# Attention units in chains: one unit's outputs and the next unit's scores in one TensorE visit, the sample tokens' attention behind all units, loads kept behind the product ahead of them

## The chip, the cores and the metric

The kernel runs on one core of a Trainium2 chip. The metric is device time in microseconds (us) of one launch. Three runs of the kernel before gave 830.59, 831.8 and 834.57 us; the median is 831.8. A core has TensorE (PE in the profile; its weight loads PEld), VectorE (DVE), ScalarE (ACT), GpSimd (POOL) and SyncE (SP, which issues most DMAs here). Each of them takes its own instructions in order.

## The reference

One layer of a hybrid decoder over 1024 prompt tokens and 8 × 4 sample tokens, width 1024. What matters here, cut from it:

```
h, gate = adaln_in(x, c, w_ada, b_ada, g_norm)            # normalised rows
(mq, mk, mv, mi, mf, mo, mz, aq, ak, av, az, gm, ga) = split_in(h @ w_in)
y_m, C, n, m = mlstm_branch(mq, mk, mv, mi, mf, mo, mz, C0, n0, m0, ...)   # chunks of 128, 4 heads
o = attention(aq, ak, av)   # 8 query heads on 2 key heads, window 128, a sink per head
y_a = o * silu(az)
u = sigmoid(gm) * (y_m @ w_mo) + sigmoid(ga) * (y_a @ w_ao)
x = x + gate * (u @ w_o)
```

Prompt attention goes in blocks of 128 tokens: a block's 128 queries see the block and the one before it. The sample tokens attend to a cache of 128 keys per sample and to themselves; their attention is a computation of its own. Their 32 rows also pass through each of the products with `w_in`.

## The kernel before, in words

**The products.** Nearly all of TensorE's time goes into `h @ w_in` and the two output products. Each fp32 operand is split into two fp32r parts (hi and lo), and each product is three fp32r matmuls with 128 × 128 weights and 288 to 512 columns. In the order of the profile: keys and values `ak`, `av` of the attention, its four groups of queries `aq`, the first four of the mLSTM heads' projections (`mq`, `mk`, `mv`) as plain products (`job`, line 569, `piece` at 525ff, tiles `g_...`), and then, from about 207 us, pairs of weight blocks in a seven-product scheme (`block_products`, line 1516, accumulators `bw`, `bx`, `by`, `bz`): the remaining head projections (`head_in`), eight pairs `ga`/`gm` (`gate`), two of `az` (`query_gate`), four of `mo`/`mz` (`head_gate`). A pair's four raw weight blocks (256 KB each, tiles `wr_...`) are loaded by its `load`; its `samples` multiplies them raw, in fp32, with the sample rows (accumulator `smp`, then `smpo`), and DVE and ACT form the split parts from them afterwards.

**What stands between the products.** Small fp32 matmuls and transposes are put between two products, in *visits*. A `Side` object (line 113) decides when. Work is written as generators that yield a lag and the names of PSUM banks ("a", "b", "o", two buffers each) that the next step needs; they run in streams, "a" (attention: at most 5 at a time, a new one 8.0 us after the last), "m" (mLSTM heads), "s" (sample attention), "g" and "x" (others). `tick` (line 140) is called after each product of a group. It has its own clock, `side.now`, which `mm` and `tr` move forward by nominal durations, lets a visit come at least 1.5 us after the last, and takes every generator whose lag is over and whose banks are free. A bank is held after a visit for `HOLD` (line 110: 2.0 us for "a" and "b", 4.0 for "o") or, where the step named "+", for 6.0 us (line 152). PE's instructions run on the chip in the order in which they are emitted (`in_order`); DVE, ACT and SP instructions of this part are placed by a scheduler that knows the data and bank dependencies, and `no_sync` (line 202) gives it an order to keep between two instructions, without a semaphore.

**An attention unit** (`unit`, line 826) is two blocks of 128 queries of one query group g, so there are 16. Its steps: four loads of queries, keys and values (tiles `uqv`, `ukv`); *scores*, 8 matmuls into two "a" banks (`sc`), behind which DVE adds the mask and takes the row maximum, four instructions, and the scores' bank is free; two yields in which ACT takes the exponentials and DVE and ACT normalise; *transposes* of the weights (`pt`, one "b" and one "o" bank); and *outputs*, 16 matmuls into an "o" bank (`oT`), behind which ACT copies them out and POOL issues the store. `queries(g)` adds the four units of a group as four generators to stream "a". From the first paired head on (`sc_bank[:] = po, "o+"` in `head_jobs`, line 1023) scores go to "o" banks, as the block products take the "a" banks, and at most three generators of stream "a" run at a time.

**Sample attention** (`sample_attention`, line 911) is one generator in stream "s": it loads the two halves of the key and value caches, transposes the keys, and does scores, softmax and outputs for the sample tokens. In the profile it stands between about 140 and 196 us. Its result `osm` is read by the `samples` step of the two `query_gate` pairs; `hook` (line 2013) holds those until all units and the sample attention are done.

**Heads.** `head` (line 1038) does one mLSTM head in groups of up to three chunks: loads `hq`, `hk`, `hv`, `et`, `qw`; `prep` (DVE: mask added to `et`, `qw` times q); transposes `tk`, `tv`; `S`; `U` with the state chain `C` on DVE; numerators `n` (also `sn` for samples).

**Loads.** `dma` calls `issue` (line 258), which puts a `dma_start` on SP. Where the scheduler puts it among SP's instructions follows from its buffer (a pool of 50 `half` tiles and pools for raw weights) and its data, so a load can stand far ahead of the product that was emitted before it.

Of the kernel before, what the change touches and what calls it, by code (L numbers as in the profile page):

```python
# [112 lines left out]
class Side:  # L113
# [26 lines left out]
    def tick(self, visit=False):  # L140
        self.each()
        for st in self.streams.values():
            if st["wait"] and len(st["live"]) < st["max"] and self.now >= st["next"]:
                self.begin(st)
        used, visit = set(), visit or self.now >= self.last + self.quiet
        for item in sorted((i for st in self.streams.values() for i in st["live"]), key=lambda i: i[1]):
            banks = set(item[2])
            if self.now < item[1] or used & banks or (banks and not visit) or any(self.now < self.free.get(b, 0) for b in banks):
                continue
            used |= banks  # L150
            for b in banks:
                self.free[b] = self.now + (6.0 if "+" in banks else HOLD[b])
            n = self.products
            self.step(item)
            if self.products > n:
                self.last = self.now
# [17 lines left out]
def body(tc, a):  # L174
    nc = tc.nc
    with ExitStack() as ctx:
# [23 lines left out]
        last = {}  # L200
# [53 lines left out]
        def dma(out, in_, late=False):  # L254
            stores(in_.tensor)
            issue(out, in_, late)

        def issue(out, in_, late=False, eng=None):
            ins = (eng or nc.sync).dma_start(out, in_)  # L259
            ins = getattr(ins, "ins", ins)  # L260
            if late:
                no_sync(ins, free)
                free.clear()
            free.append(ins)
# [556 lines left out]
        osm = cp.tile([128, NH, NS], F32, name="osm")  # L821
        yaD = [dp.tile([128, T], F32, name=f"yaD{g}") for g in range(4)]

        sc_bank = [pa, "a"]

        def unit(g, b0):
            sink = at["sink"]
            los = [128 if b == 0 else 0 for b in (b0, b0 + 1)]
            n0 = 1 if b0 == 0 else 0
            qv, kv_ = ht([128, 4, 128], "uqv"), ht([128, 4, 128], "ukv")  # L830
            q, kT = qv[:, 0:2].rearrange("p c e -> p (c e)"), kv_[:, 0:3].rearrange("p c e -> p (c e)")
            vn = kv_[:, 3], qv[:, 2], qv[:, 3]
            dma(q, qD[g][:, b0 * 128:b0 * 128 + 256])
            dma(kT[:, n0 * 128:], kD[:, (b0 - 1 + n0) * 128:(b0 + 2) * 128])
            dma(qv[:, 2:4], vnD[:, b0:b0 + 2])
            if b0:
                dma(vn[0], vnD[:, b0 - 1])
            yield 12.0, sc_bank[1]
            p = [ht([128, 2, 256], f"p{kv}") for kv in range(2)]
            mx = sm([128, 4], "mx", 3)  # L840
            scs = [sc_bank[0]([128, 2, 256], f"sc{g}_{b0}_{kv}") for kv in range(2)]
            for i, lo in enumerate(los):
                qc, kc = slice(i * 128, i * 128 + 128), slice(i * 128 + lo, i * 128 + 256)
                for kv, r in enumerate(half_rows):
                    mm(scs[kv][:, i, lo:], q[r, qc], kT[r, kc], start=True, stop=True, share=2)
            for kv in range(2):
                for i, lo in enumerate(los):
                    V.tensor_tensor_reduce(p[kv][:, i, lo:], scs[kv][:, i, lo:], amask[:, lo:], 1.0, sink[:, kv, g:g + 1],
                                           ALU.add, ALU.max, accum_out=mx[:, 2 * kv + i:2 * kv + i + 1])
            nmx = sm([128, 8], "nmx", 3)  # L850
            V.tensor_scalar(nmx[:, 0:4], mx, -1.0, None, op0=ALU.mult)
            v2 = lambda t: t.rearrange("p (k i) -> p k i", i=2)
            V.tensor_tensor(v2(nmx[:, 4:8]), sink[:, :, g:g + 1].to_broadcast((128, 2, 2)), v2(mx), op=ALU.subtract)
            yield 2.5, ""
            den = sm([128, 4], "den", 3)
            S.activation(nmx[:, 4:8], nmx[:, 4:8], AF.Exp)
            for kv in range(2):
                for i, lo in enumerate(los):
                    j = 2 * kv + i
                    S.activation(p[kv][:, i, lo:], p[kv][:, i, lo:], AF.Exp, bias=nmx[:, j:j + 1],  # L860
                                 accum_out=den[:, j:j + 1])
            yield 3.0, ""
            V.tensor_tensor(den, den, nmx[:, 4:8], op=ALU.add)
            V.reciprocal(den, den)
            for kv in range(2):
                for i, lo in enumerate(los):
                    j = 2 * kv + i
                    if kv:
                        S.activation(p[kv][:, i, lo:], p[kv][:, i, lo:], AF.Copy, scale=den[:, j:j + 1])
                    else:  # L870
                        V.tensor_scalar(p[kv][:, i, lo:], p[kv][:, i, lo:], den[:, j:j + 1], None, op0=ALU.mult)
            yield 7.6, "b"
            pT = [t.rearrange("p i (j e) -> p (i j) e", e=128) for t in p]
            for kv in range(2):
                pt = (pb, po)[kv]([128, 4, 128], f"pt{g}_{b0}_{kv}")
                for j in range(n0, 4):
                    tr(pt[:, j], p[kv][:, j // 2, j % 2 * 128:j % 2 * 128 + 128], ident)
                if kv:
                    V.tensor_copy(pT[kv][:, n0:], pt[:, n0:])
                else:  # L880
                    S.copy(pT[kv][:, n0:], pt[:, n0:])
            yield 5.0, "o"
            oT = po([128, 2, 128], f"oT{g}_{b0}")
            for j in range(n0, 4):
                i, hf = divmod(j, 2)
                for kv in range(2):
                    r = slice(64 * kv, 64 * kv + 64)
                    mm(oT[r, i], vn[i + hf][:, r], pT[kv][:, j], start=(hf == 0 or b0 + i == 0), stop=(hf == 1))
            c0 = b0 * 128
            o = qv[:, 0:2].rearrange("p c e -> p (c e)")  # L890
            S.copy(o, oT.rearrange("p c e -> p (c e)"))
            issue(oD[g][:, c0:c0 + 256], o, eng=nc.gpsimd)
            units_done.append((g, b0))

        def queries(g):
            cs = at["rope"]

            def ev_q(p, acc, c0, n):
                q = ht([128, 384], "aq")[:, :n]
                S.activation(q, acc[:, :n], AF.Copy, scale=0.125)  # L900
                t = rope(q, cs[p], n, ht([128, 384], "aqr"), qD[g], c0)
                if p == 2:
                    v3 = lambda x, r: x[r, 256:288].rearrange("p (b t) -> p b t", t=NT)
                    for kv, r in enumerate(half_rows):
                        V.tensor_tensor(at["qpad"][r, :, kv, g], v3(q, r), v3(t, r), op=ALU.add)

            job(("aq", g), ev_q)
            for b0 in (0, 2, 4, 6):
                side.add("a", unit(g, b0))

        def sample_attention():
            qpad, vns, kTs = at["qpad"], at["vns"], at["kTs"]
            kc, vc = ([ht([128, 4, 128], f"{n}{u}") for u in range(2)] for n in ("kc", "vc"))
            smask = ht([128, 2, WIN + NS], "smask")
            sinkr = cp.tile([128, 1], F32, name="sinkr")
            for u in range(2):
                dma(kc[u], a["cache_k"][:, 4 * u:4 * u + 4])
                dma(vc[u], a["cache_v"][:, 4 * u:4 * u + 4])
            dma(smask, a["smask"])
            dma(sinkr, a["sink_rows"])  # L920
            yield 12.0, "b"
# [27 lines left out]
            V.reciprocal(den, den)  # L949
            for u in range(2):  # L950
                V.tensor_scalar(p[:, u], p[:, u], den[:, u:u + 1], None, op0=ALU.mult)
            yield 10.0, "b"
            pt = pb([128, 4, 128], "pts")
            for u in range(2):
# [45 lines left out]
        def head_jobs(h):  # L1000
# [15 lines left out]
            for n, dst, smp, scale in (("mq", q, qs, float(128 ** -0.5)), ("mk", k, ks, 1.0), ("mv", v, vs, 1.0)):  # L1016
                if (n, h) not in order:
                    return
                i = order.index((n, h)) - order.index(None)
                if i == -1:  # L1020
                    plain_ends.append(True)
                    side.finish("g")
                    sc_bank[:] = po, "o+"
                    side.streams["a"]["max"] = 3
                    next(work)
                job((n, h), keep(dst, smp, scale, "s"), (lambda: next(work)) if i == -1 else None)
                head_part(h, 2)
# [901 lines left out]
        side.add("m", gates(gp, zg, gbias), "")  # L1929
        side.add("a", kv_turn(), "b")  # L1930
        V.on = S.on = False

        gbD, gsD = dp.tile([1, D], F32, name="gbD"), dp.tile([NS, D], F32, name="gsD")

# [78 lines left out]
        def hook(n, i):  # L2013
# [9 lines left out]
                side.add("x", att_sums(LOADS.index((n, i))))  # L2023
            if n == len(pairs) - 1:
                next(att, None)

        OUT_WEIGHTS = 5
        LOADS = [(len(pairs) - 2, 7), (len(pairs) - 1, 5)]
# [348 lines left out]
```

## Time and profile before

| | us |
|---|---|
| median of three runs | 831.8 |
| the profiled execution | 830.97 |
| its span (first to last instruction) | 829.2 |
| DVE busy | 592.7 |
| ACT busy | 420.6 |
| POOL busy | 67.5 |
| DMA, mean over the span | 186 GB/s |

The mean granted TensorE clock of the profiled execution was 0.996 of full speed. A row of a timeline reads: start, duration, engine, line, operation, out<-in, the shape of the weight tile (rows\*columns of the array), the moving operand, count; in brackets, idle time of the engine just before and what ended it. A matmul's duration overlaps the next one's, so its cost is read from start to start. L271 and L276 are the lines of the helpers `mm` and `tr`, L220 that of DVE, ACT and POOL calls, L259 that of DMA issues, so groups are told apart by their tiles.

### The profile page before, as it was taken

How to read it: one execution, taken by the hardware profiler on the slowest of the kernel's cores; microseconds unless marked ns; L12 is line 12 of the kernel's file. 1: busy time of each engine (PE TensorE's matmuls, PEld its weight loads, DVE VectorE, ACT ScalarE, POOL GpSimd, SP SyncE). 2: the span in 40 equal slices, each digit the busy share in tenths (PEclk: the TensorE clock that was granted, in tenths of full speed). 3: DMA queues.
4: the chain of work that ended last, by engine and by line, in shares of the span. 5: the costliest groups of instructions: out<-in, count | busy, mean ns of one | idle time of the engine just before them, and what ended most of it. 6: DMA issues, size and time to landing. Idle time of an engine off the chain costs nothing. (4 is left out here: it accounts for less than half of the span.)

```text
span 829.2 us, 15039 instructions
## 1 busy us (share of the span) xinstructions
PE 810.1 (98%) x5129; PEld 670.8 (81%) x5129; DVE 592.7 (71%) x1479; ACT 420.6 (51%) x1030; POOL 67.5 (8%) x128
## 2 busy tenths in 40 slices
PE   6999999999999999999899999999999999999996
PEld 3779897888788788888788878888888789987775
DVE  4889886647556456475567786797669988964776
ACT  5664365565474564555455454554446654334343
POOL 0120000000000001000001010000002104250000
PEclk9999999999999999999999999999999999999999
DMA  9997756346435324468756354464336785543533
GB/s 332 379 359 239 200 186 212 118 151 219 141 111 186 118 81 150 139 242 279 256 191 211 105 169 150 147 205 142 103 120 197 228 295 186 191 146 123 202 109 108
DMA packets 106689, 153.96 MB, mean 186 GB/s; under 512 B 20448, under 2 KB 54368, under 8 KB 106580
## 3 DMA queue, kind: packets, MB, share of 16 engines
q1 hardware_dynamic: 100964, 142.25, 52.2%
q10 hardware_dynamic: 4176, 6.56, 2.2%
q0 software_dynamic: 1472, 4.20, 1.4%
q8 instruction: 40, 0.66, 0.3%
q14 instruction: 37, 0.30, 0.1%
HBM read 109.22 MB, written 44.75 MB: 186 GB/s over the span
## 5 line engine op out<-in xcount | busy, mean ns | idle before, releaser
L220 ACT ACTIVATE p<-p,nmx 128x256 f32<-128x256 f32 (+1 forms) x64 | 31.0, 485 | 12.4 <-DVE nmx L220 12.1
L271 PE MATMUL g_aq<-h_h,wh_aq 128*128 128x384 f32 (+1 forms) x96 | 32.2, 336 | 0.0
L271 PE MATMUL g_aq<-h_h,wl_aq 128*128 128x384 f32 (+1 forms) x96 | 30.9, 322 | 0.0
L271 PE MATMUL g_aq<-h_l,wh_aq 128*128 128x384 f32 (+1 forms) x96 | 30.8, 321 | 0.0
L271 PE MATMUL g_w_mo<-ym_l,wh_w_mo 128*128 128x384 f32 (+1 forms) x96 | 30.8, 321 | 0.0
L271 PE MATMUL g_w_mo<-ym_h,wh_w_mo 128*128 128x384 f32 (+1 forms) x96 | 30.8, 321 | 0.0
L271 PE MATMUL g_w_mo<-ym_l,wl_w_mo 128*128 128x384 f32 (+1 forms) x96 | 30.8, 321 | 0.0
L220 DVE CUSTOM_DVE_ANT_0 p<-sc,cst,sink 128x256 f32<-128x256 f32 (+1 forms) x64 | 26.2, 464 | 5.3 <-PE sc L271 5.2
L259 POOL DMA_DIRECT2D oD<-uqv x16 | 8.9, 554 | 183.2 <-ACT uqv L220 161.0
L220 DVE COPY p<-pt 128x512 f32<-128x512 f32 (+1 forms) x16 | 10.5, 656 | 13.6 <-PE pt L276 13.6
L271 PEld LDWEIGHTS g_aq<-h_h,wh_aq 128*128 128x128 f32 x96 | 18.0, 188 | 2.5 <-issue 1.5
L271 PEld LDWEIGHTS g_w_mo<-ym_l,wh_w_mo 128*128 128x128 f32 x96 | 18.0, 188 | 0.0
L271 PEld LDWEIGHTS g_aq<-h_l,wh_aq 128*128 128x128 f32 x96 | 18.0, 188 | 0.0
L271 PEld LDWEIGHTS g_w_mo<-ym_h,wh_w_mo 128*128 128x128 f32 x96 | 18.0, 188 | 0.0
L271 PE MATMUL sc<-ukv,uqv 64*128 64x256 f32 (+1 forms) x128 | 18.0, 390 | 0.0
L271 PEld LDWEIGHTS g_w_mo<-ym_l,wl_w_mo 128*128 128x128 f32 x96 | 18.0, 188 | 0.0
L271 PEld LDWEIGHTS g_aq<-h_h,wl_aq 128*128 128x128 f32 x96 | 18.0, 188 | 0.0
L220 ACT ACTIVATE p<-p,den 128x256 f32<-128x256 f32 (+1 forms) x32 | 14.5, 491 | 5.7 <-DVE den L220 5.6
L220 DVE TENSOR_TENSOR et<-et,S 128x384 f32<-128x384 f32 (+1 forms) x12 | 6.1, 510 | 15.6 <-PE S L271 12.9
L220 ACT ACTIVATE sq<-rows_h 128x512 f32<-128x512 f32 (+2 forms) x14 | 8.2, 582 | 17.8 <-issue 12.0
L271 PE MATMUL g_mq<-h_h,wh_mq 128*128 128x384 f32 (+1 forms) x48 | 16.8, 349 | 0.3 <-ACT mk L220 0.3
L276 PE MATMUL pt<-cst,p 128*128 128x128 f32 x120 | 16.4, 277 | 0.5 <-DVE mx L220 0.5
(2073 smaller groups left out, 2842.4 us busy)
## 6 DMA issues: line engine op xcount, KB each, us to landing
x<-xT SPq DMA_DIRECT2D x16, 256.0 KB, 5.4
early_h<-w_ada SPq DMA_DIRECT2D x8, 512.0 KB, 9.0
adar_ga<-w_ada SPq DMA_DIRECT2D x16, 256.0 KB, 3.9
wr_ga<-w SPq DMA_DIRECT2D x16, 256.0 KB, 2.9
wr_gm<-w SPq DMA_DIRECT2D x16, 256.0 KB, 3.0
taD<-gt SPq DMA_DIRECT2D x16, 256.0 KB, 2.0
tmD<-gt SPq DMA_DIRECT2D x16, 256.0 KB, 5.5
wor<-w_out SPq DMA_DIRECT2D x16, 256.0 KB, 4.9
```

Of the source, the lines that this page charges most:

```text
L220: ins = f(*args, **kw)
L259: ins = (eng or nc.sync).dma_start(out, in_)
L271: in_order(nc.tensor.matmul(out, lhsT, rhs, start=start, stop=stop, skip_group_check=more))
L276: in_order(nc.tensor.transpose(out, in_, idn))
```

## The change

It changes six things and no arithmetic.

- `queries` no longer adds four generators per group; it appends four units to a list, and for g = 0, 1, 2 adds one *chain* to stream "a".
- A chain (`unit_chain`, new) runs units one after another. When a unit's transposes are done and the list holds another unit, the chain takes it and starts it (its loads go out), and then does the outputs of the first and the scores of the second in one step, which asks for the banks of both; what remains is the second unit's steps. The third chain takes no new unit once the paired heads have begun.
- Outputs that share a visit go to `sc_bank[2]`: an "o" bank as before, and a "b" bank once the scores themselves go to "o" banks.
- The 6.0 us of hold for "+" now hold for bank "o" alone, not for the other bank of the same visit.
- `sample_attention` waits until all 16 units are done; it issues the loads of the value cache only behind its softmax, no longer with those of the keys.
- From the end of the attention's keys and values to the start of the second pair from the end, each load on SP gets a `no_sync` order behind the last PE instruction emitted before it (`paced`).

In the two programs' orders, the scores of the first unit stand where they stood, 13 visits hold `oT` and `sc` one behind the other (none before), the last `oT` stands near 300 us of a nominal count (319 before), and sample attention near 324 to 365 us.

```
-                self.free[b] = self.now + (6.0 if "+" in banks else HOLD[b])
+                self.free[b] = self.now + (6.0 if b == "o" and "+" in banks else HOLD[b])
...
+        paced = []
+
         def issue(out, in_, late=False, eng=None):
             ins = (eng or nc.sync).dma_start(out, in_)
             ins = getattr(ins, "ins", ins)
+            if eng is None and paced:
+                no_sync(ins, [last["PE"]])
...
-        sc_bank = [pa, "a"]
-
-        def unit(g, b0):
+        sc_bank = [pa, "a", po, "o"]
+        units = []
+
+        def unit(g, b0, joined):
...
             yield 5.0, "o"
-            oT = po([128, 2, 128], f"oT{g}_{b0}")
+            oT = (sc_bank[2] if joined else po)([128, 2, 128], f"oT{g}_{b0}")
...
+        def unit_chain(i):
+            v = w = None
+            while v or len(units_done) < 16:
+                if v is None:
+                    if not units or (i == 2 and plain_ends):
+                        yield 1.0, ""
+                        continue
+                    joined = []
+                    v = unit(*units.pop(0), joined)
+                    next(v)
+                    yield 12.0, sc_bank[1]
+                yield next(v)
+                yield next(v)
+                step = next(v)
+                if units and not (i == 2 and plain_ends):
+                    after = []
+                    w = unit(*units.pop(0), after)
+                    next(w)
+                    joined.append(True)
+                yield step
+                lag, _ = next(v)
+                yield lag, sc_bank[1] + sc_bank[3] if w else "o"
+                for _ in v:
+                    pass
+                v, w = w, None
+                if v:
+                    joined = after
+
...
             for b0 in (0, 2, 4, 6):
-                side.add("a", unit(g, b0))
+                units.append((g, b0))
+            if g < 3:
+                side.add("a", unit_chain(g))
 
         def sample_attention():
             qpad, vns, kTs = at["qpad"], at["vns"], at["kTs"]
-            kc, vc = ([ht([128, 4, 128], f"{n}{u}") for u in range(2)] for n in ("kc", "vc"))
+            while len(units_done) < 16:
+                yield 1.0, ""
+            kc = [ht([128, 4, 128], f"kc{u}") for u in range(2)]
...
                 dma(kc[u], a["cache_k"][:, 4 * u:4 * u + 4])
-                dma(vc[u], a["cache_v"][:, 4 * u:4 * u + 4])
...
+            vc = [ht([128, 4, 128], f"vc{u}") for u in range(2)]
+            for u in range(2):
+                dma(vc[u], a["cache_v"][:, 4 * u:4 * u + 4])
...
-                    sc_bank[:] = po, "o+"
+                    sc_bank[:] = po, "o+", pb, "b"
...
         V.on = S.on = False
+        paced.append(True)
...
+            if n == len(pairs) - 2:
+                paced.clear()
```

## Prediction

> **What bounds the kernel now.** I read the page's first part, then the waits of TensorE (PE), then windows, then the timeline where the windows show a dip.
>
> ```profile
> span 829.2 us, 15039 instructions
> PE 810.1 (98%) x5129; PEld 670.8 (81%) x5129; DVE 592.7 (71%) x1479; ACT 420.6 (51%) x1030; POOL 67.5 (8%) x128
> ```
>
> PE is busy for 810.1 of 829.2 us; no other engine passes 71%. So the time is what PE's instructions take in the order they stand in, plus its stalls. The waits (in total, times, longest) give the stalls:
>
> ```profile
> PE S L271 <- DVE C L220: 2.3, 1, 2.3
> PE bw L271 <- ACT bw L220: 0.7, 1, 0.7
> PE pt L276 <- DVE mx L220: 0.5, 1, 0.5
> PE g_mq L271 <- ACT mk L220: 0.3, 1, 0.3
> ```
>
> Apart from the start, which the change doesn't touch, these four are nearly all of it. Windows (PE is the first busy column; granted clock, DMA share and GB/s stand last) show what the first of them cost:
>
> ```profile
> 100.00:120.00 20.00, 20.00 (x138) 17.98 (x138) 18.44 (x71) 10.31 (x32) 0.71 (x1) 1.00 0.61 197
> 180.00:200.00 20.00, 19.98 (x189) 15.96 (x186) 12.36 (x44) 9.99 (x33) 1.31 (x4) 1.00 0.69 221
> 402.00:408.00 6.00, 3.74 (x25) 3.38 (x24) 1.85 (x4) 1.73 (x8) 0.10 (x1) 0.90 0.69 242
> 408.00:412.00 4.00, 4.00 (x15) 3.17 (x14) 2.32 (x4) 2.22 (x5) 0.00 (x0) 0.72 0.57 210
> ```
>
> PE is full elsewhere (the first two rows). From 402 to 408 it idles for 6.00 − 3.74 = 2.26 us, and the granted clock then falls: 0.90 over 6 us loses 0.60 us, 0.72 over 4 us loses 1.12. The dip cost 2.26 + 0.60 + 1.12 = **4.0 us**.
>
> **The change part by part.** PE gets the same 5129 instructions. In the two programs' instruction orders, set side by side, only their places differ, with those of the loads. So there are three terms: visits of small fp32 groups that merge or split, stalls that go, stalls that come.
>
> *Merged visits.* A visit interrupts the fp32r products. Scores alone, then outputs alone (start, duration, both in us):
>
> ```profile
> 122.60 0.34 PE L271 MATMUL g_mq<-h_h,wl_mq 128*128 128x384 f32 x1
> 122.87 1.13 PE L271 MATMUL sc<-ukv,uqv 64*128 64x256 f32 x8
> 123.94 0.44 PE L271 MATMUL g_mq<-h_h,wh_mq 128*128 128x384 f32 x1
> 124.22 0.33 PE L271 MATMUL g_mq<-h_l,wh_mq 128*128 128x384 f32 x1
> ```
>
> ```profile
> 126.32 0.33 PE L271 MATMUL g_mq<-h_l,wh_mq 128*128 128x384 f32 x1
> 126.49 0.34 PE L271 MATMUL g_mq<-h_h,wl_mq 128*128 128x384 f32 x1
> 126.76 0.44 PE L271 MATMUL oT<-p,ukv 128*64 128x128 f32 x4
> 127.03 0.83 PE L271 MATMUL oT<-p,uqv 128*64 128x128 f32 x12
> 127.78 0.44 PE L271 MATMUL g_mq<-h_h,wh_mq 128*128 128x384 f32 x1
> 128.06 0.33 PE L271 MATMUL g_mq<-h_l,wh_mq 128*128 128x384 f32 x1
> ```
>
> Product to product is 0.17 us (126.32 to 126.49). The step into either group is 0.27 and the first step after it 0.28. So each border costs 0.10, and two visits have four borders. Two groups put into one visit:
>
> ```profile
> 143.73 1.07 PE L271 MATMUL ada_ga<-adar_ga,c 128*32 128x512 f32 x8
> 144.73 1.14 PE L271 MATMUL sc<-ukv,uqv 64*128 64x256 f32 x8
> 145.79 0.44 PE L271 MATMUL g_mk<-h_h,wh_mk 128*128 128x384 f32 x1
> ```
>
> Scores behind other matmuls take 145.79 − 144.73 = 1.06; alone they take 123.94 − 122.87 = 1.07. The inner border is free, and a merge saves two borders, 0.2 us. After the change 13 visits hold outputs and the next unit's scores; before none does. No row shows that pair, so I take 0.2 from the nearest one, with 0 as the lower end and 0.4 (all four borders) as the upper. Three merges of the sample sums with numerators, or of like kind, are lost: −13 × 0.2 + 3 × 0.2 = **−2.0 us**.
>
> Some 14 lost adjacencies have transposes at one side, and these I price at nothing:
>
> ```profile
> 132.31 0.34 PE L271 MATMUL g_mq<-h_h,wl_mq 128*128 128x384 f32 x1
> 132.48 1.04 PE L276 MATMUL pt<-cst,p 128*128 128x128 f32 x8
> 133.44 0.93 PE L271 MATMUL sc<-ukv,uqv 64*128 64x128 f32 x8
> ```
>
> Products enter transposes in 0.17 us, the plain step, so a visit of transposes alone has no border to pay at its front. If I am wrong by 0.05 each, it is 0.7 us.
>
> One page speaks against this term. The Trainium skill, "TensorEngine Tiling (Array Packing)", section "Key Properties", says that a change of tiling mode (the tile shapes behind the "*" above) drains TensorE. By that rule outputs (128\*64) to scores (64\*128) is a switch as well; two visits have four switches and the merged one three, so the 13 merges would save half. The row of 144.73 disagrees, as 128\*32 to 64\*128 cost nothing there; but no run here shows this pair.
>
> *The stall at 404 goes.* Its cause, DVE's and SP's instructions ahead of S:
>
> ```profile
> 404.54 0.56 DVE L220 TENSOR_TENSOR et<-et,cst 128x384 f32<-128x384 f32 x1 [2.07 <-DMA et<-nmd]
> 405.92 0.56 DVE L220 TENSOR_TENSOR qw<-qw,hq 128x384 f32<-128x384 f32 x1 [0.83 <-DMA qw<-wid]
> 406.40 0.34 DVE L220 SCALAR_TENSOR_TENSOR C<-C,dec,U 128x129 f32<-128x129 f32 x1
> ```
>
> ```profile
> 398.84 0.32 SPq L259 DMA_DIRECT2D et<-nmd  x1
> 399.25 0.38 SPq L259 DMA_DIRECT2D qw<-wid  x1
> ```
>
> S needs the bank that C reads last; C stands in DVE's order behind two preparations whose loads were issued at 398.84 and 399.25, and which started at 404.54 and 405.92: 5.7 and 6.7 us from issue to use. In the changed order C still stands behind such a pair, but their loads come about 13 us before S needs the bank (they came 404.4 − 398.84 = 5.5 us before). 13 is above 6.7, so the wait goes: −4.0. What is late next there is the visit after it, counted below. The two smaller waits go too, as their visits no longer stand like that: pt (−0.5, transposes right behind scores whose bank they need) and g_mq (−0.3). Together **−4.8 us**.
>
> *New stalls.* Side by side, nine places remain where PE's next group follows what it waits for with less room than its chain took before: scores at the end of the key products, where DVE is full (18.44 of 20 us in the row of 100 to 120); one visit with outputs, scores and transposes like the one of 0.5; head products behind evictions on ACT and DVE; three numerator visits around 390 to 400; and the first sample sums. The four rows of waits above show what such places cost when they cost anything: 0.3 to 0.7 leaving out the big one. I take 0.3, the lowest, as several will be covered: 9 × 0.3 = **+2.7 us**; ends 0 and 9 × 0.7 = 6.3.
>
> *Loads placed behind the product ahead.* SP's issues are tied to the last PE instruction in program order. For the gate weights this cuts the lead:
>
> ```profile
> L271 PE MATMUL smp<-wr_gm,c x128: 272/273/297, 308.9 to 486.8; 128*32 128x128 f32 x128
> ```
>
> ```profile
> L259 SPq DMA_DIRECT2D wr_gm<-w x16: 328/333/424, 275.7 to 467.0; - x16
> wr_gm<-w SPq DMA_DIRECT2D x16, 256.0 KB, 3.0
> tmD<-gt SPq DMA_DIRECT2D x16, 256.0 KB, 5.5
> wor<-w_out SPq DMA_DIRECT2D x16, 256.0 KB, 4.9
> ```
>
> ```profile
> 401.92 0.39 PE L271 MATMUL bw<-t2h,wh_pgate__4792 128*128 128x512 f32 x1
> 402.15 0.39 PE L271 MATMUL bw<-t2l,wh_pgate__4792 128*128 128x512 f32 x1
> ```
>
> Before, the first load goes out at 275.7 for sums at 308.9 (33 us), the last at 467.0 for 486.8 (20 us). After, by the order, a pair's last load stands 15 products (15 × 0.23 = 3.5 us, by the rows of 401.92 and 402.15) ahead of its sums at two visits (near 407 and 567 us), some 4.3 us at a third, 5.6 at a fourth, and 6 to 11 at the others. A load takes 3.0 us to land, so I count nothing beyond the 0.3 above. Loads amid others took 4.9 and 5.5, and the four of a pair now go out within 2 to 3 us of each other: that is the slower rival. The same tie takes loads out of the first 100 us, where no stall of PE is put down to a load: nothing.
>
> *Sample attention* moves from about 140 to 196 us to about 324 to 365. Its result is first needed with the query gates, after 500 us, so it costs its visits only, as before; the unit work ends some 20 us earlier, in windows where DVE has room (12.36 of 20 from 180 to 200). The freed hold on a bank, the split cache loads: nothing, since no PE instruction is added. If that cover failed, scores would wait on DVE, which the first of the nine places prices.
>
> **The sum.** 830.97 (profiled execution; 829.2 of span and 1.8 around it) − 2.0 − 4.8 + 2.7 = 826.9. The median of the runs, 831.8, lies 0.8 above that execution; I add half of it: **827.3 us**. What can be told from no change is about 0.5%, so faster begins at 827.6 and slower at 836.0.
>
> **Rivals.**
> *A, my forecast*, 825 to 829.5: new stalls between 0.5 and 5 us.
> *B, merges save nothing*: +0.6 instead of −2.0, so 829.9. For it: no row of this pair; against: the row of 144.73. The page's rule lies halfway, 828.6, inside A.
> *C, the big stall comes back* at another numerator visit, since DVE still takes preparations and C in order: 827.3 + 4.0 = 831.3. For it: the same instructions, still in one order; against: the 13 us of lead. This is the case in which the change does not do what it seems to.
> *D, slower: late gate weights.* Each pair's four loads share the engines, and the last lands last. If it takes 6.0 us, the four visits with the least lead stall 2.5, 2.5, 1.7 and 0.4 us, 7.1 together, and two of these idles are as long as the one at 404 and bring its slow clock (0.60 + 1.12 each): 827.3 + 7.1 + 3.4 = 837.8. Below some 5.7 us of landing it stays inside 0.5%. For it: 4.9 and 5.5 beside these loads; against: 3.0 as their own median, and SP isn't held by PE when it runs, so that it may be ahead of its place in the order.
> *E, no new stall*: 827.3 − 2.7 = 824.6, and 822.6 if a merge saves 0.4.
>
> On D's price, the Trainium skill, "TensorE: Matmul & The Clock Gate", section "What's actually happening", has the clock halve after an idle window of about 3.4 us. The trace disagrees on the length: 2.26 us of idle was enough here.
>
> **Chances.** A 0.43, E 0.20, D 0.17, B 0.10, C 0.10. Faster: all of E and 0.24 of A, 0.44. Same: the rest of A, B, C and 0.02 of D, 0.41. Slower: 0.15 of D. The range runs from 823.5 (E with part of the larger saving) to 835.0, leaving out D and the low end of E.
>
> **What would show it.** In the changed trace: outputs and scores in one visit with the scores' part at about 1.07 us (B: 1.2 or more with the step behind it); no wait of S on C near 400; waits of PE in a list of parts of 0.2 to 0.7, 2 to 3 us in total; smp without a wait on DMA. A wait of smp on wr_gm or wr_ga, or a granted clock below 1.00 between 300 and 490, would make it wrong toward D; a PE wait above 2 us in any other place, toward C.

## The result, and the profile after

The changed kernel takes **836.4 us** in the median (835.48 to 838.18, 8 runs); the kernel before, measured beside it, 831.65 (829.35 to 834.57). The ratio is 1.0061, 95% interval 1.0046 to 1.0077: it is slower by 0.6%, clear of noise. The forecast of 827.3 us missed in size and in sign, and the time lies above its range, which ended at 835.0.

The page of the changed kernel, span and busy time:

```profile
span 834.5 us, 15050 instructions
PE 811.4 (97%) x5129; PEld 671.0 (80%) x5129; DVE 591.1 (71%) x1479; ACT 418.9 (50%) x1030; POOL 68.0 (8%) x128
```

TensorE still has the same 5129 instructions and is busy nearly throughout; the span grew by 5.3 us. Its waits (total, times, longest), those above 0.2 us without the start:

```profile
PE bw L275 <- ACT bw L220: 3.3, 2, 2.6
PE pt L280 <- DVE mx L220: 2.8, 2, 2.1
PE bx L275 <- ACT gt L220: 1.0, 1, 1.0
...
PE by L275 <- DVE gt L220: 0.5, 1, 0.5
PE smp L275 <- DMA wr_gm<-w: 0.4, 2, 0.3
```

The wait of S on C is gone, as forecast. In its place stand one of 2.6 us (bw, near 529 us) and one of 2.1 (transposes pt, near 256), and a few smaller ones. The wait at 256 brought the slow clock, that is a stretch with a granted clock below 1.00, as the wait at 404 did before (granted clock in the third column from the right):

```profile
256.00:260.00 4.00, 3.25 (x13) 2.65 (x14) 2.95 (x12) 1.76 (x5) 0.00 (x0) 0.76 0.17 66
260.00:264.00 4.00, 4.00 (x22) 3.49 (x21) 0.97 (x4) 3.66 (x15) 0.10 (x1) 0.82 0.00 0
520.00:540.00 20.00, 17.40 (x119) 13.36 (x117) 13.96 (x32) 8.89 (x20) 0.00 (x0) 1.00 0.45 142
```

0.24 and 0.18 of 4 us each are 1.7 us lost behind the idle time; at 529 the clock stayed full (third row). The merged visit, one of 13:

```profile
187.23 0.34 PE L275 MATMUL g_mq<-h_h,wl_mq 128*128 128x384 f32 x1
187.50 0.44 PE L275 MATMUL oT<-p,ukv 128*64 128x128 f32 x4
187.76 0.83 PE L275 MATMUL oT<-p,uqv 128*64 128x128 f32 x12
188.52 1.14 PE L275 MATMUL sc<-ukv,uqv 64*128 64x256 f32 x8
189.58 0.44 PE L275 MATMUL g_mq<-h_h,wh_mq 128*128 128x384 f32 x1
189.87 0.34 PE L275 MATMUL g_mq<-h_l,wh_mq 128*128 128x384 f32 x1
```

The scores take 189.58 − 188.52 = 1.06 us here too: the border from outputs to scores costs nothing. Above plain steps of 0.17 the visit costs 189.87 − 187.23 − 0.34 = 2.30 us. The two visits of before (122.60 to 124.22, 126.49 to 128.06) cost 1.28 + 1.23 = 2.51. So a merge saves 0.21.

Where the 5.3 us of span come from, each item from the waits, the timeline and the windows of the two traces (a visit is priced against the cheapest showing of the same visit in any run; the two totals of the first line are such sums, which no view shows; what counts is their difference):

| | us |
|---|---|
| visits, all of them, at their cheapest: 142.5 before, 140.8 after | −1.7 |
| the wait at 404 and its slow clock | −4.0 |
| the waits of pt at 288 and g_mq at 136 | −0.8 |
| transposes at 256: wait 2.1, restart 0.2, slow clock 1.7 | +4.0 |
| bw at 529 | +2.6 |
| bx at 367 | +1.0 |
| numerators, S and by, 398 to 410 | +1.1 |
| sample sums at 416 | +1.2 |
| scores and transposes at 122 and 181 | +1.4 |
| start, up to the first product | +0.3 |
| sum | +5.1 |

0.2 us are left over. So the expected gains came, 6.5 us of them, and 11.3 us of new stalls ate them.

### The profile page after: what moved, and what is told of

Its sections match the earlier page's. It is cut to its first block, busy times and chain, and to the rows that moved or that the text cites. A ratio compares the mean times of both kernels' runs of the same rounds, so it can differ in the third digit from the quotient of the medians.

```text
span 834.5 us, 15050 instructions
## 1 busy us (share of the span) xinstructions
PE 811.4 (97%) x5129; PEld 671.0 (80%) x5129; DVE 591.1 (71%) x1479; ACT 418.9 (50%) x1030; POOL 68.0 (8%) x128
## 5 line engine op out<-in xcount | busy, mean ns | idle before, releaser
L220 DVE COPY p<-pt 128x512 f32<-128x512 f32 (+1 forms) x16 | 10.5, 655 | 10.9 <-PE pt L280 10.8
L280 PEld LDWEIGHTS pt<-cst,p 128*128 128x128 f32 x120 | 13.8, 140 | 4.9 <-DVE mx L220 3.3
```

The source lines that it names most:

```text
L220: ins = f(*args, **kw)
L280: in_order(nc.tensor.transpose(out, in_, idn))
```

## The experiments

Two theories at the outset. **Collisions**: the new order puts groups of TensorE right behind unfinished work of VectorE and ScalarE, and each place is a matter of a few products. **Late loads**: the tie of the loads to the product ahead is what costs. All times are medians, with the ratio to the kernel before measured beside it. Waits and rows are those of one profiled execution of each run.

### Parts alone and parts undone

**No tie.** Edit:

```
-        paced.append(True)
```

> The changed kernel with the loads no longer tied to the product ahead of them; TensorE's order is that of the changed kernel. Collisions (the new order puts groups right behind unfinished work of VectorE and ScalarE; loads have little to do with it): the waits at 256 (2.1 us and a slow clock of 1.8) and at 529 (2.6) stay, only the sums' waits on their weights go (0.4 shown, about 1 in all): 834.5 to 836.5. Late loads (the tie is what costs): most of the 4.8 us over the kernel before goes: 831 to 832, and below that by the merges.

832.1 us, ratio 1.0018 (1.0005 to 1.0030). Inside the changed kernel the tie costs some 4 us, so the forecast by collisions missed. The wait at 256 stayed, though (1.9 us, without the slow clock this time, which is 1.7 of the 4 in the two traces), and that of 2.6 at 529 became two of 1.0 and 0.9. The waits of bx, by and the sums on their weights are gone without the tie.

**The tie alone**, in the kernel before:

```
+            if eng is None and paced:
+                no_sync(ins, [last["PE"]])
...
         V.on = S.on = False
+        paced.append(True)
...
+            if n == len(pairs) - 2:
+                paced.clear()
```

> The kernel before with the loads tied to the product ahead and nothing else; TensorE's order is that of before. Collisions: the waits of before, with up to 1.5 us for sums that wait for weights: 831 to 833.5. Late loads: 835 to 837, with waits of smp or of evictions that before has not.

829.1 us, ratio 0.9970 (0.9958 to 0.9982): the tie alone **gains** 2.6 us. Neither theory had that. The instructions ahead of S, on SP and on VectorE, in this run:

```profile
405.64 0.32 SPq L261 DMA_DIRECT2D et<-nmd  x1
406.06 0.73 SPq L261 DMA_DIRECT2D qw<-wid  x1
```

```profile
405.60 0.69 DVE L220 TENSOR_TENSOR ws<-wr_gm,wr_gm 128x512 f32<-128x512 f32 x1
406.20 0.34 DVE L220 SCALAR_TENSOR_TENSOR C<-C,dec,U 128x129 f32<-128x129 f32 x1
...
408.65 0.56 DVE L220 TENSOR_TENSOR et<-et,cst 128x384 f32<-128x384 f32 x1 [0.27 <-DMA et<-nmd]
```

The loads of et and qw go out at 405.64 and 406.06, later than before (398.84 and 399.25), so their preparations fall behind C, and C no longer waits for a transfer. S waits 0.4 us and not 2.3. The stall at 404 was a matter of VectorE's order, and a later load cured it. So late loads, as a cause by itself, falls: what the tie does depends on the order that it meets.

**The old hold**, 6.0 us for both banks:

```
-                self.free[b] = self.now + (6.0 if b == "o" and "+" in banks else HOLD[b])
+                self.free[b] = self.now + (6.0 if "+" in banks else HOLD[b])
```

> The changed kernel with the hold of 6.0 us for both banks, as before the change. In its order the transposes no longer come 9 products behind a visit with outputs and scores near 256, and the sample head's steps near 529 stand 12 products earlier. Collisions: 256 goes (2.1 + 1.8) and 529 goes wholly or in part (2.6), with 0 to 3 us of other waits: 829 to 833. Late loads: the tie is the same, so 835 to 837.

830.5 us, ratio 0.9994 (0.9978 to 1.0010), as collisions had it. The transposes at 256 and the eviction at 529 no longer wait. TensorE near 256 in the changed kernel, then VectorE there, then VectorE in this run:

```profile
250.86 1.13 PE L275 MATMUL sc<-ukv,uqv 64*128 64x256 f32 x8
...
254.10 0.60 PE L280 MATMUL pt<-cst,p 128*128 128x128 f32 x4
256.75 0.66 PE L280 MATMUL pt<-cst,p 128*128 128x128 f32 x4 [2.06 <-DVE mx L220]
```

```profile
254.59 0.69 DVE L220 TENSOR_TENSOR mkv<-p,by 128x512 f32<-128x512 f32 x1 [3.31 <-DMA qD<-mkv]
255.80 0.48 DVE L220 CUSTOM_DVE_ANT_0 p<-sc,cst,sink 128x256 f32<-128x256 f32 x1 [0.53 <-DMA oD<-uqv]
```

```profile
256.79 0.69 DVE L220 TENSOR_TENSOR mkv<-p,by 128x512 f32<-128x512 f32 x1 [3.61 <-DMA qD<-mkv]
257.50 0.49 DVE L220 CUSTOM_DVE_ANT_0 p<-sc,cst,sink 128x256 f32<-128x256 f32 x1
```

VectorE stands 3.3 us before the buffer of `mkv`, which a store still reads, and the row maxima of the scores stand behind it; the scores hold the "o" bank that the second half of the transposes needs. The transposes come nine products behind the scores, at 254.10, since the freed hold lets them take the "b" bank of the outputs so soon. With the old hold VectorE waits just as long (3.61), but the transposes come later and TensorE doesn't feel it. By the addresses in the two programs, laid over the traces, all 50 buffers of the `half` pool are in use at 250 us, and some 44 to 48 there in the kernel before; no view shows this count. What came instead here: some 3.3 us near 410 (the sums wait for wr_gm, by behind them) and its slow clock.

**Sample attention behind the eighth unit** (`while len(units_done) < 8`):

> The changed kernel with the sample tokens' attention started behind the eighth unit and not the sixteenth. From there on the order is dealt anew: near 256 and 529 as in the run with the hold put back. Collisions: both waits go, with 0 to 3 us of others: 829 to 833. Late loads: 835 to 837.

834.9 us, ratio 1.0037 (1.0021 to 1.0052); both expectations miss. The waits at 256 and 529 went, but S waits 1.9 us at 264, with the slow clock, and the sums at 411 with what follows 3.4. An order dealt anew brings its own collisions.

### Which loads, and the buffers

**The pairs' weights untied**, in the changed kernel:

```
+                        tied, paced[:] = paced[:], []
                         dma(t, a["w1"][JOBS[n]][:, 4 * kh:4 * kh + 4])
+                        paced[:] = tied
```

> The changed kernel with the four weight loads of each pair no longer tied; all other loads stay tied, TensorE's order is that of the changed kernel. Late pair weights (through the tie a pair's weights stand on SyncE behind loads that wait for a buffer, and their splits fall among the evictions): the waits of smp at 416, of bx at 367 and the large one at 529 go or shrink, 830.5 to 832.5. Tie as a whole (other loads matter as much): 834 to 836. In both the wait at 256 stays, as no pair load has part in it.

838.7 us, ratio 1.0084 (1.0052 to 1.0116): worse, against both. The sums no longer wait, but bx waits 2.4 us and not 1.0, and two stalls have the slow clock. ScalarE ahead of bx:

```profile
393.59 0.60 ACT L220 ACTIVATE gt<-bx 128x512 f32<-128x512 f32 x1 [5.31 <-DMA woDp<-wor]
```

It waits 5.3 us for a buffer that a store of w_out's rows still reads. That the sooner weights slow this store isn't shown; no run tells it apart.

**The same with the old hold**:

> The changed kernel with the old hold and the pairs' weight loads untied. Late pair weights: of the run with the old hold alone (830.5) the wait of smp near 410 (3.5 us with what it delays), that of by behind it (1.4) and the slow clock there (1.8) go: 824 to 826. If these waits only change places: 829 to 832.

829.6 us, ratio 0.9979 (0.9964 to 0.9994), the second branch: the waits changed places. ScalarE waits 3.9 us before a buffer of w_out's rows, and TensorE 3.2 behind it.

**The kernel before, tied but for the pairs' weights**:

> The kernel before with all loads tied except the pairs' weights. If the tie gained (829.1 with all loads tied) because the other loads, those of w_out above all, no longer go out among the head's et and qw: the gain stays and the wait of smp at 383 (1.4) goes, 827 to 828.5. If it gained because the pairs' weights came later and left the engines to et and qw: S waits at 404 again, 831 to 832.5.

828.4 us, ratio 0.9968 (0.9954 to 0.9983): the first branch by its time. What gained in the tie was the other loads, et and qw among them: here too the preparation of et (408.17) stands behind C (404.30). That w_out's loads matter in it, as the branch had it, isn't shown.

**The old hold without the tie**:

> The changed kernel with the old hold and no load tied: chains, merged visits and the later sample attention alone. Late pair weights: 824 to 827, as with only the pairs untied, and up to 4 us more if S waits for et and qw again. If the waits only change places: 829 to 832.

829.3 us, ratio 0.9974 (0.9960 to 0.9987). Chains, merged visits and the later sample attention alone gain 2.3 us; the waits changed places again (numerators 1.5 us at 418).

**The old hold, the pairs untied, w_out's rows one lot at a time**. Edit beside the two known:

```
-            ahead = [load(lots[0])]
             yield 5.0, ""
             for i, ks in enumerate(lots):
-                raws = ahead.pop()
-                if i + 1 < len(lots):
-                    ahead.append(load(lots[i + 1]))
-                yield 3.0, ""
+                raws = load(ks)
+                yield 6.0, ""
```

> The run with the old hold and the pairs untied (829.6), with the rows of w_out loaded one lot at a time. There ScalarE stood 3.9 us before a buffer that a store of these rows still read, and TensorE 3.2 us behind it. Full pool: that wait goes, 826 to 827. If not: 829 to 830.5.

827.7 us, ratio 0.9949 (0.9933 to 0.9965), between the two branches. The wait of 3.2 us is gone, as the full pool had it. The edit frees two to four buffers and thins the traffic as well; the two aren't told apart, but the rows of w_out are shown as its cause.

**The same, tied only from the paired heads on** (`paced.append(True)` moved to the place where `plain_ends` is set):

> The run of 827.7 (old hold, pairs untied, w_out one lot at a time) with the tie beginning at the paired heads and no longer at the end of the keys. If the early tie makes the first scores wait for their keys (0.9 us at 92): 826.5 to 827.2. If that wait comes from elsewhere: 827.5 to 828.5.

827.0 us, ratio 0.9945 (0.9926 to 0.9964). The wait of the first scores on their keys is gone: the early tie caused it.

### The stalls of the changed kernel, one by one

**256: the transposes of one unit later** (two lags of unit (3, 2)):

```
-            yield 7.6, "b"
+            yield 7.6 + 4.5 * ((g, b0) == (3, 2)), "b"
...
-            yield 5.0, "o"
+            yield 5.0 - 5.0 * ((g, b0) == (3, 2)), "o"
```

> The changed kernel with one lag longer: the transposes of unit (3, 2) come 21 products later, behind the head's visit, and a dozen later visits shift by 3 to 12 products; from product 1022 on TensorE's order is the same. Collisions: the wait of 2.1 us at 256 and its slow clock of 1.8 go and nothing comes for them: 832 to 833. If stalls only change places: 835 to 837.

834.9 us, ratio 1.0032 (1.0021 to 1.0043), a gain of 0.3% on the changed kernel where 0.4 to 0.5% was expected. In the trace the stall and its clock went: TensorE's fp32r products counted from the first, this run stands 2.5 us behind the changed kernel at product 850 and 1.4 ahead at 950, which is 3.9. The 2.5 are of its first 160 us (1.0 at the start, then small waits for loads), where the edit changes nothing.

**529, a first try: ScalarE's casts emitted later** (lags of sample head 2 by +3.0 and −3.0):

> The changed kernel with the casts of one sample head (h = 2) emitted 3.0 us later and its next step as much sooner, so that TensorE's order is the same to the last instruction. Collisions: the eviction that bw waits for at 529 no longer stands behind those casts, 2.6 us go: 833.5 to 834.5. If it is another chain that holds that eviction: 836 to 837.

837.4 us, ratio 1.0059 (1.0038 to 1.0079). The edit did nothing: the scheduler put the casts where they had been, ahead of the eviction, so this run tests neither branch. It tells one thing beside that, in the last section.

**529, a second try: the casts ordered behind**, with `not_before(S)` around them and 6.0 us later:

> The changed kernel with the casts of the sample head h = 2 ordered behind ScalarE's evictions near 529 (6.0 us later and an order that is kept); the visits up to product 1784 are the same, four later ones stand 3 to 15 products later. Casts ahead of the evictions as the cause: the wait of 2.6 at 529 goes, 833 to 834.5. VectorE's chain as the cause: it stays, 836 to 837.

835.9 us, ratio 1.0055 (1.0038 to 1.0073). The wait is 2.0 us and not 2.6, so ordering the casts behind took 0.6 off it, and VectorE is the next to be tried. Its rows, changed kernel first, then the kernel before:

```profile
526.15 0.42 DVE L220 TENSOR_TENSOR vf<-sz,wm 32x258 f32<-32x258 f32 x1
526.60 0.55 DVE L220 TENSOR_TENSOR vm<-vf,vm 32x388 fp32r<-32x388 f32 x1
527.18 0.29 DVE L220 CAST vm<-vf 32x258 fp32r<-32x258 f32 x1
527.48 0.69 DVE L220 TENSOR_TENSOR gt<-p,bw 128x512 f32<-128x512 f32 x1
```

```profile
519.24 0.69 DVE L220 TENSOR_TENSOR gt<-p,bw 128x512 f32<-128x512 f32 x1 [0.99 <-PE bw L271]
519.85 0.68 DVE L220 TENSOR_TENSOR wl_pquery_gate__6266<-wr_az,wh_pquery_gate__6265 128x512 fp32r<-128x512 f32 x1
520.45 0.17 DVE L220 TENSOR_TENSOR sz<-sxb,cst 32x32 f32<-32x32 f32 x1
```

`gt<-p,bw` reads the bank bw and lets ScalarE refill it. Before, it stood ahead of the sample head's chain; after, behind it, since that head's visit came 6 products sooner.

**529, the chain itself ordered behind the eviction**:

```
+            if h == 2:
+                yield 5.0, ""
...
+                with not_before(*([V] if h == 2 else [])):
```

> The changed kernel with VectorE's chain of the sample head h = 2 (three broadcasts of its values and what hangs on them) behind the eviction near 529; TensorE's order is the same to the last instruction. VectorE's chain as the cause: the wait of 2.6 at 529 goes wholly, 833 to 834.5. If something else holds the eviction: 2.0 or more stay, 835.5 to 837.

832.6 us, ratio 1.0019 (1.0004 to 1.0035): the wait is gone, and with the order on TensorE unchanged the cause of the stall at 529 is shown. The median lies a little below the branch of 833 to 834.5; in the profiled execution the place at 529 gave 2.9 us, counted by products, and 1.9 more came at 256, where the wait of 1.7 had no slow clock.

**367, 398 to 410 and 416: w_out's rows one lot at a time**, with the later transposes and the first try on the casts:

> Both of these edits at once, and the rows of w_out loaded one lot at a time and not one lot ahead, which frees two to four buffers of the pool of 50 between 360 and 440 us and keeps SyncE from standing before a full pool. TensorE's order is that of the run with the later transposes. Full pool as the cause of the waits at 367, 398 to 401 and 416 (3.5 us together): 826.5 to 828.5. If these have other causes: 829.5 to 831.

831.25 us, ratio 0.9991 (0.9978 to 1.0004). None of these waits is left in the trace, so the rows of w_out caused them under the tie (without the tie they were gone as well). The time meets neither branch: the expected one had counted on the casts, and the 2.6 of 529 are still there: 831.25 − 2.6 = 828.65, still a little above the 828.5.

**All repairs**, that is the later transposes, w_out's rows one lot at a time and, for 529, first the casts ordered behind, then VectorE's chain:

> The changed kernel with the three repairs together: the transposes of one unit later, the rows of w_out one lot at a time, the casts behind the evictions. If these stalls are the loss: 836.4 less 3.9 (256 and its slow clock), 3.5 (367, 398 to 401, 416) and 2.6 (529) is 826.4; 826 to 828. If new ones come in their place: 829.5 to 832.

829.2 us, ratio 0.9976 (0.9960 to 0.9991); 2.0 us and the slow clock stay at 529 (522 in this run).

> The changed kernel with three repairs: the transposes of one unit later, the rows of w_out one lot at a time, VectorE's chain behind the eviction. If the stalls found are the loss: 836.4 less 3.9, 3.5 and 2.6 is 826.4; 826 to 828. If new ones come in their place: 829 to 831.

826.8 us, ratio 0.9943 (0.9922 to 0.9965), beside an expected 826.4. All waits of TensorE in that run:

```profile
PE xc L275 <- ACT xsq L220: 6.2, 1, 6.2
PE pt L280 <- DVE mx L220: 0.7, 1, 0.7
PE sc L275 <- DMA ukv<-kD: 0.7, 1, 0.7
PE adat_q L275 <- ACT adas_q L220: 0.7, 1, 0.7
PE xc L275 <- ACT xsum L220: 0.7, 1, 0.7
PE bw L275 <- ACT bw L220: 0.7, 1, 0.7
PE smp L275 <- DVE sz L220: 0.2, 1, 0.2
```

The stalls found, 10.0 us by the expectation, make up the loss: the run lies 9.6 us below the changed kernel.

**The same, tied only from the paired heads on**:

> The kernel of 826.8 with the three repairs, with the tie beginning at the paired heads. If the early tie makes the first scores wait for their keys (0.7 us): 825.5 to 826.5. If not: 826.5 to 827.5.

826.0 us, ratio 0.9924 (0.9911 to 0.9937): the wait of sc is gone. This version beats both kernels: it takes 6.3 us less than the one before beside it, and 1.4% less than the changed one (0.9924 / 1.0061). No run has w_out's rows one lot at a time in the kernel before, so how much of the 6.3 us that edit would give without the change stays open.

## Why the prediction was wrong, point by point

**Merged visits: right.** A merge saved 0.21 us where 0.2 was taken, and all visits together 1.7 where 2.0 was. The rival that merges save nothing is out. So is the saving of half that was worked out from the rule of the Trainium skill ("TensorEngine Tiling (Array Packing)", "Key Properties"): 188.52 to 189.58 shows no time lost to a drain from 128\*64 to 64\*128.

**The stall at 404 goes: right, and for the reason given** as far as it went: et and qw were issued at 389.22 and 389.64 and prepared at 390.08 and 391.02, and C ran at 399.70. The run with the tie alone adds that a later load does it as well, since then their preparations stand behind C.

**The two small waits: right** (0.8 us).

**Loads cost nothing, late weights as the slower rival: the mechanism occurred, at one visit, and its size didn't decide.** The sums at 416 lost 1.2 us, not the 10.5 of the rival. SP's rows, then the sums:

```profile
405.30 2.81 SPq L261 DMA_DIRECT2D wor<-w_out  x4
408.16 0.43 SPq L261 DMA_DIRECT2D wr_ga<-w  x1
410.43 0.33 SPq L261 DMA_DIRECT2D wor<-w_out  x1
410.81 0.90 SPq L261 DMA_DIRECT2D wr_gm<-w  x2
```

```profile
416.52 0.41 PE L275 MATMUL smp<-wr_gm,c 128*32 128x128 f32 x2 [0.19 <-DMA wr_gm<-w]
417.18 0.30 PE L275 MATMUL smp<-wr_gm,c 128*32 128x128 f32 x1 [0.25 <-DMA wr_gm<-w]
```

A load of w_out's rows stood before a full pool, and wr_gm behind it in SP's order. Its two loads went out at 410.81 and 411.29 for sums that began at 415.92, more than the 3.5 us ahead that the prediction had for this visit. But the sums that waited for them ran 5.7 and 5.9 us behind the issue, near the 6.0 that the rival took and far from the 3.0 of the forecast. With one lot at a time (and the later transposes) the loads went out from 398.53 on, 12 us ahead, and the wait on them is gone. So SP held up and a slow landing came together here. The rival's second visit, near 567, had its weights 12 us ahead (547.1 for 559.3) and no wait. The rival's threshold was also off: by its own sum it stays inside 0.5% up to some 5.5 us of landing, not 5.7.

**New stalls: the step that failed.** It said nine places at 0.3 us, 2.7 in all, with 6.3 as the upper end. They cost 11.3. Four places fit its list (122, 181, 398 to 410, 416) and cost 3.7 together; 256, 367 and 529 don't and cost 7.6. The price was taken from rows in which TensorE waits for an eviction of one or two instructions. At 256 and 529 it waited for a chain: VectorE before a buffer that a store still read, or a dozen small instructions of the sample head. And the price left out the slow clock, though the prediction had just counted it at 404. Two places at the price of that row (2.26 + 1.7) in place of 0.3 each would have put the sum at 827.3 − 0.6 + 7.9 = 834.6. The rival that the big stall comes back had this price, but for a numerator visit and with a chance of 0.10; by the prediction's own sign, a wait above 2 us in another place, the trace went toward it.

**The freed hold on a bank: put at nothing, and wrong too.** The reason given was that TensorE gets no instruction more. With the old hold the changed kernel takes 830.5 us and not 836.4, and untied 829.3 and not 832.1. Of the three parts that were undone alone this one gains the most: 5.9 us, the tie 4.3, the sample attention's place 1.5. At 256 the freed hold lets the transposes in before VectorE is done; at 529 the old hold moves the sample head's visit 12 products. In part this is luck of the order, since the old hold brought its own stall near 410.

Cover was reckoned by engines (VectorE has room), while the 50 buffers, all in use at 250 us in the changed kernel, were not counted at all.

## What to carry to other kernels

When TensorE is full and a change only moves work, count what each moved group waits for down to the last engine, and the buffers that the waiting instruction needs: a free engine in front of a full pool is no cover. Price a possible new stall by the longest one in the trace with its clock, not by the commonest. And undo the parts one by one: here the tie alone and the chains alone (with the old hold) each gained 2 to 3 us, while the whole change lost 5 until three places were set right.

## What the runs showed of the hardware

The slow clock followed idle time unreliably in these runs. The eviction at 529 kept TensorE idle for 2.60 us in the changed kernel and again in the run with ScalarE's casts emitted later, whose order on TensorE is the same. In the first the granted clock stayed at 1.00 (row of 520 to 540 above), in the second:

```profile
528.00:532.00 4.00, 2.37 (x8) 1.91 (x9) 2.61 (x5) 1.87 (x4) 0.00 (x0) 0.84 0.53 165
532.00:536.00 4.00, 4.00 (x15) 3.09 (x13) 0.69 (x1) 1.10 (x2) 0.00 (x0) 0.73 0.57 167
```

Of the other runs, one had the slow clock after 1.9 us of idle time (S at 264, with sample attention behind the eighth unit: 0.57 from 268 to 272), and one kept 1.00 after 3.2 (by at 413, the old hold with the pairs untied). The Trainium skill, "TensorE: Matmul & The Clock Gate", section "What's actually happening", says that the window of the clock gate runs freely, so that it matters where in it an event falls; these rows are in keeping with that, though no run shows the window itself. Its figure of a whole idle window of about 3.4 us as the condition they don't bear out. A stall of 2 us was thus worth 2 or nearly 4 here.
